# Strassen-type weight sums turned into additions, two of the four in the first MLP matrix made by accumulating DMA transfers

## Chip, cores and metric

The kernel runs on one core of one Trainium2 chip. The metric is the device time of one execution in microseconds (us), the median of three runs. A profiled execution gives the traces quoted below; its times are those of that one execution.

## What is computed

One decoder layer on a sequence of 512 tokens with 2048 channels, all in float32:

```
h = rmsnorm(x, g_mix)
z = h @ w_in                     # 2048 x 10248: conv B, C, V | Q, K, V | forget logits | two gates
conv_branch = (cb * causal_dwconv(cc * cv, conv_w)) @ w_conv_out
attn_branch = forgetting_attention(q, k, v, log_f) @ w_attn_out
merged = sigmoid(gate_c + b) * conv_branch + sigmoid(gate_a + b) * attn_branch
x = x + merged @ w_mix_out
h = rmsnorm(x, g_mlp)
u = square(relu(h @ w_ff1))      # w_ff1: 2048 x 8192
x = x + u @ w_ff2                # w_ff2: 8192 x 2048
out = rmsnorm(x, g_final)
```

## The kernel before

**Products.** Every float32 product is made from float32r parts: an operand is split into a high part (`th`, by ScalarE, line 101) and the rest (`tl`, by VectorE, line 102), and TensorE multiplies high by high, rest by high, and high by rest. A split of one 128 x 2048 tile is therefore one ScalarE and one VectorE instruction, in this order, and TensorE starts a product when `th` is there and needs `tl` for its last third. There are two `th` and two `tl` buffers, so that a split can run at most two products ahead of TensorE.

**Seven products for eight.** The matrix `w_in` (class `Group`, from line 164), `w_ff1` (the same class through `ff1`, line 720) and `w_ff2` (function `unit`, line 770) are multiplied by the Strassen-Winograd scheme: each block of weights is cut into four quarters `X[i, j]`, and seven products named A11, A12, S4, S2, S3, S1 and A22 take the place of eight. Four of the seven weight operands are sums of quarters, made by VectorE in place, 128 x 2048 each (lines 240 to 244 in `Group.tail`): first `X00 = X01 - X00`, then `X01 = X11 - X01`, then `X11 = X11 - X00` (the operand of S2) and `X10 = X10 - X11` (the operand of A22). The second is the operand of S3, the first that of S1. The matching sums of the activations are made in `Quarters.sums` (line 368), and for the second MLP matrix in `put_u` (lines 691 to 698), where the squared activations are combined in seven arrays `r`, split into `rh` and `r`, and stored to DRAM in `s_d` (lines 703, 704).

**A group.** One `Group` is 2 x 256 columns of weights. `head` loads X00 and X10 and makes A11 and A12; `tail` loads X01 and X11 and makes S4, S2, S3, S1, A22. The quarters have four SBUF slots of 1 MiB, handed on through the list `free`: the next group's X00 takes the slot of X11, its X10 that of X01, its X01 that of X00, its X11 that of X10, each as soon as the last split that reads it is done. All these loads are issued by SP (line 178), in the order X00, X10, X01, X11. For `w_ff1` there are 16 groups: four heads first (while the token blocks are still being normalised), then their four tails, then twelve whole groups. `later` holds work that a group leaves to the next tail.

**POOL's queue** carries, in the `w_ff1` stage, the writes and reads of `c_d` (lines 710, 689: a quarter of the activations that is kept in DRAM for a while) and the stores to `s_d`, two pairs of 896 KB for each group. `r` and `rh` have one buffer each, so the next set of sums waits until the store before it has landed.

**Order.** The program is written engine by engine in program order, and a scheduler of the framework then moves instructions within an engine's queue; each engine runs its queue in order.

Of the kernel before, what the change touches and what calls it, by code (L numbers as in the profile page):

```python
# [8 lines left out]
F32 = mybir.dt.float32  # L9
# [3 lines left out]
ALU = mybir.AluOpType  # L13
AX = mybir.AxisListType

P = 128
S = 512
# [3 lines left out]
HS = S // 2  # L21
# [14 lines left out]
V1W = (AW // 2 + NH) // 2  # L36
QSCALE = float(P) ** -0.5
WBUF, SHIFT, PAD = 33 * 64, 16, 16


ORDER = ("A11", "A12", "S4", "S2", "S3", "S1", "A22")
# [4 lines left out]
def tile_hybrid_block(ctx: ExitStack, tc, x, g_mix, w_in, b_f, b_gate, conv_w, w_conv_out,  # L46
                      w_attn_out, w_mix_out, g_mlp, w_ff1, w_ff2, g_final, out):
    nc = tc.nc
    x, out = x[0], out[0]
    w_in, w_conv_out, w_attn_out, w_mix_out = w_in[0], w_conv_out[0], w_attn_out[0], w_mix_out[0]  # L50
    w_ff1, w_ff2 = w_ff1[0], w_ff2[0]
# [3 lines left out]
    main = ctx.enter_context(tc.tile_pool(name="main", bufs=1))  # L55
# [10 lines left out]
    def pair(i, dt, name):  # L66

        return main.tile([P, 2, D], dt, tag=f"t{i}", name=name)
# [35 lines left out]
    def sub(out, a, b):  # L104
        nc.vector.tensor_tensor(out=out, in0=a, in1=b, op=ALU.subtract)  # L105

    def add(out, a, b):
        nc.vector.tensor_tensor(out=out, in0=a, in1=b, op=ALU.add)  # L108

    def parts(shape, at=0):  # L110

        q, w = shape[1:]
        return tuple(main.tile([P, WBUF], F32R, tag=tag, name=tag, bufs=2)[:, at:at + q * w]
                     .rearrange("p (q c) -> p q c", q=q) for tag in ("th", "tl"))
# [49 lines left out]
    class Group:  # L164

        def __init__(self, view, c1, c2, w, ST, mm, banks, put, scale=1.0):
            self.view, self.cs, self.w, self.ST, self.mm, self.banks = view, (c1, c2), w, ST, mm, banks
            self.put, self.scale, self.at = put, scale, {}  # L170

        def load(self, i, j):

            t = main.tile([P, KT // 2, self.w], F32, tag=f"x{free[0]}", name=f"x{i}{j}")
            self.at[i, j] = free.pop(0)
            c = self.cs[j]
            src = self.view[:, c:c + self.w].rearrange("(q two p) c -> two p q c", two=2, p=P)
            nc.sync.dma_start(out=t, in_=src[i])
            return t

        def acc(self, which):
            return [bank(i, which) for i in self.banks["abcd".index(which)]]
# [16 lines left out]
        def plus(self, s, ps, scale=1.0):  # L199

            if len(ps) == 1:
                pairs = [(s, ps[0][:, :2 * self.w].rearrange("p (b c) -> p b c", b=2))]
            else:
                pairs = [(s[:, b, :], ps[b][:, :self.w]) for b in range(2)]
            for o, p in pairs:
                if scale == 1.0:
                    add(o, p, o)
                else:
                    nc.vector.scalar_tensor_tensor(out=o, in0=p, scalar=scale, in1=o, op0=ALU.mult, op1=ALU.add)

# [18 lines left out]
        def tail(self):  # L229
            if self.at:  # L230
                X = self.X
            else:
                X = {(i, 0): self.load(i, 0) for i in range(2)}
            X[0, 1], X[1, 1] = self.load(0, 1), self.load(1, 1)
            a = self.a
            c = self.acc("c")
            self.run(c, "S4", X[1, 1], True)
            while later:
                later.pop(0)()
            sub(X[0, 0], X[0, 1], X[0, 0])  # L240
# [85 lines left out]
    class Quarters:  # L326
# [353 lines left out]
    def put_u(g):  # L680
# [5 lines left out]
        def sums(j):  # L686
            r = pf.tile([P, 7, HS], F32, tag="r", name="r")
            if j == 0:
                nc.gpsimd.dma_start(out=r[:, 0:6:5], in_=c_d[g])
# [10 lines left out]
            nc.scalar.activation(out=h, in_=r, func=AF.Copy)  # L700
            nc.vector.tensor_tensor(out=r, in0=r, in1=h.bitcast(F32), op=ALU.subtract)
            q = 2 * (g % 2) + j
            nc.gpsimd.dma_start(out=s_d[g // 2][:, :, 0, q, :], in_=h.bitcast(F32))
            nc.gpsimd.dma_start(out=s_d[g // 2][:, :, 1, q, :], in_=r)
# [65 lines left out]
    def unit(seg, cg, ST):  # L770
# [4 lines left out]
            kept[cg] = banks2(2 + cg, "b")  # L775
        b = kept[cg]
        X, at = {}, {}
        for i, j in ((0, 0), (0, 1), (1, 1), (1, 0)):
            at[i, j] = free.pop(0)
            t = main.tile([P, 4, S], F32, tag=f"x{at[i, j]}", name=f"y{i}{j}")  # L780
            c = NW * cg + S * j
            src = w_ff2[seg * 1024:(seg + 1) * 1024, c:c + S].rearrange("(q two p) c -> two p q c", two=2, p=P)
            nc.sync.dma_start(out=t, in_=src[i])
            X[i, j] = t

        def run(ps, n, src, first):
            hi, lo = parts([P, 4, S])
# [98 lines left out]
```

## Time and profile before

| | us |
|---|---|
| median of 3 runs | 2563.29 (2560.9 to 2570.82) |
| the profiled execution, whole | 2564.2 |
| its span, first to last instruction | 2562.5 |
| TensorE busy | 2470.4 |
| VectorE busy | 1910.2 |
| ScalarE busy | 1117.7 |

"Busy" is the time in which an engine has an instruction under way. A window of the trace gives, for a stretch of the span, each engine's busy time with its instructions in brackets, the clock granted to TensorE as a share of full speed, the busy share of the sixteen DMA engines and the rate at which they moved bytes. A timeline row gives start, duration, engine, line, operation, output and inputs, and in square brackets how long the engine stood idle before it and what released it. A load from `w_ff1` is 1 MiB and its tile is called `x`; in `w_ff2` it is called `y`. The `w_ff1` stage runs from about 1245 us to 1912 us of the span: heads to 1285, the four tails to 1418.6, the twelve whole groups after that.

### The profile page before, as it was taken

To read this page: it belongs to the slowest core of one execution; us is meant where nothing else is said; L and a number is where in the kernel's file an instruction comes from. 1 tells how busy PE (TensorE), PEld (TensorE's weight loads), DVE (VectorE), ACT (ScalarE), POOL (GpSimd) and SP (SyncE) were. 2 spreads that over 40 slices of the span, in tenths; PEclk is the share of its full clock that TensorE was granted. 3 is DMA by queue.
4 is the path that set the end of the run, shared out by engine and by line. 5 is a ranking of instruction groups with operands and counts; after the bars stand their busy time and mean duration, and the time that the engine had idled before them with its cause. 6 is when DMAs were issued, how large, how long until landed. Compare 5 with 4: busy or idle time off the path is not lost. (4 is left out here: it accounts for less than half of the span.)

```text
span 2562.5 us, 39034 instructions
## 1 busy us (share of the span) xinstructions
PE 2470.4 (96%) x16957; PEld 2267.2 (88%) x16957; DVE 1910.2 (75%) x1484; ACT 1117.7 (44%) x1060; POOL 113.3 (4%) x166
## 2 busy tenths in 40 slices
PE   8999999999999999999998999999989999999997
PEld 8999899999999988888988999999987787787875
DVE  7877677788776744335887888788878878778787
ACT  6433433344454522224545555555543333333344
POOL 0000000000000000000001111111111000000000
PEclk9999999999999999999999999999999999999999
DMA  7554443457344544535656575756687565655562
GB/s 239 168 195 146 144 136 124 147 190 231 126 144 153 199 142 143 184 109 204 207 180 224 192 238 186 235 182 213 205 322 248 191 241 201 230 171 183 205 223 89
DMA packets 292383, 479.75 MB, mean 187 GB/s; under 512 B 10140, under 2 KB 200692, under 8 KB 286452
## 3 DMA queue, kind: packets, MB, share of 16 engines
q1 hardware_dynamic: 268096, 345.08, 41.8%
q0 software_dynamic: 23248, 131.08, 13.6%
q8 instruction: 133, 2.18, 0.3%
q10 hardware_dynamic: 868, 1.10, 0.1%
q14 instruction: 38, 0.31, 0.0%
HBM read 380.75 MB, written 96.47 MB: 186 GB/s over the span
## 5 line engine op out<-in xcount | busy, mean ns | idle before, releaser
L102 DVE TENSOR_TENSOR tl<-x,th 128x2048 fp32r<-128x2048 f32 (+1 forms) x252 | 575.8, 2289 | 192.3 <-ACT th L101 175.1
L101 ACT ACTIVATE th<-x 128x2048 fp32r<-128x2048 f32 (+1 forms) x252 | 481.9, 1917 | 469.3 <-PE a L138 155.3
L105 DVE TENSOR_TENSOR x<-x,x 128x2048 f32<-128x2048 f32 (+1 forms) x144 | 329.4, 2287 | 41.3 <-DMA x<-in_w_ff_dram 35.0
L136 PE MATMUL a<-S,th 128*128 128x256 f32 x1088 | 262.4, 285 | 33.1 <-ACT th L101 27.3
L101 ACT ACTIVATE th<-y 128x2048 fp32r<-128x2048 f32 x80 | 153.8, 1923 | 287.0 <-DVE y L105 115.7
L138 PE MATMUL a<-S,th 128*128 128x256 f32 x1088 | 259.6, 282 | 0.0
L136 PEld LDWEIGHTS a<-S,th 128*128 128x128 f32 x1088 | 210.1, 193 | 38.0 <-ACT th L101 31.6
L102 DVE TENSOR_TENSOR tl<-y,th 128x2048 fp32r<-128x2048 f32 x80 | 182.8, 2285 | 46.1 <-ACT th L101 46.1
L102 DVE TENSOR_TENSOR tl<-raw,th 128x2048 fp32r<-128x2048 f32 x40 | 91.7, 2293 | 160.4 <-ACT th L101 160.0
L138 PEld LDWEIGHTS a<-S,th 128*128 128x128 f32 x1088 | 210.1, 193 | 0.1
L154 PE MATMUL a<-th,us 128*128 128x512 f32 x512 | 202.3, 395 | 8.0 <-DMA us<-s_d 6.2
L156 PE MATMUL a<-th,us 128*128 128x512 f32 x512 | 200.4, 391 | 0.0
L101 ACT ACTIVATE th<-raw 128x2048 fp32r<-128x2048 f32 x40 | 76.8, 1921 | 193.6 <-PE pt L293 71.4
L136 PE MATMUL c<-S,th 128*128 128x256 f32 x544 | 129.4, 282 | 10.0 <-ACT th L101 10.0
L158 PE MATMUL a<-tl,us 128*128 128x512 f32 x512 | 137.8, 391 | 1.1 <-DVE tl L102 1.1
L140 PE MATMUL a<-S,tl 128*128 128x256 f32 x1088 | 138.4, 278 | 0.0
L140 PEld LDWEIGHTS a<-S,tl 128*128 128x128 f32 x1088 | 130.1, 188 | 0.6
L138 PE MATMUL c<-S,th 128*128 128x256 f32 x544 | 128.7, 281 | 0.0
L136 PE MATMUL b<-A,th 128*128 128x256 f32 x544 | 126.2, 277 | 1.5 <-ACT th L101 1.4
L154 PEld LDWEIGHTS a<-th,us 128*128 128x128 f32 x512 | 96.8, 189 | 34.8 <-ACT th L101 15.0
L138 PE MATMUL d<-S,th 128*128 128x256 f32 x544 | 126.8, 278 | 0.0
L136 PE MATMUL d<-S,th 128*128 128x256 f32 x544 | 126.7, 278 | 0.0
(221 smaller groups left out, 5842.1 us busy)
## 6 DMA issues: line engine op xcount, KB each, us to landing
x<-in_w_in_dram SPq DMA_DIRECT2D x86, 1024.0 KB, 5.7
x<-in_w_ff_dram SPq DMA_DIRECT2D x72, 1024.0 KB, 7.6
y<-in_w_ff_dram SPq DMA_DIRECT2D x64, 1024.0 KB, 6.3
us<-s_d POOLq DMA_DIRECT2D x24, 2048.0 KB, 9.9
s_d<-rh POOLq DMA_DIRECT2D x32, 896.0 KB, 6.7
s_d<-r POOLq DMA_DIRECT2D x32, 896.0 KB, 8.1
raw<-in_w_mix_out_dram SPq DMA_DIRECT2D x24, 1024.0 KB, 5.0
g_d<-o SPq DMA_DIRECT2D x32, 256.0 KB, 2.2
```

The costliest lines, as they stand in the source:

```text
L101: nc.scalar.activation(out=hi, in_=src, func=AF.Copy)
L102: nc.vector.tensor_tensor(out=lo, in0=src, in1=hi.bitcast(F32), op=ALU.subtract)
L105: nc.vector.tensor_tensor(out=out, in0=a, in1=b, op=ALU.subtract)
L136: nc.tensor.matmul(o, hi[:, q, js], Sx[:, 0, q, :], start=first and q == 0 and j == 0, stop=False, skip_group_check=True)
L138: nc.tensor.matmul(o, hi[:, q, js], Sx[:, 1, q, :], start=False, stop=False, skip_group_check=True)
L140: nc.tensor.matmul(o, lo[:, q, js], Sx[:, 0, q, :], start=False, stop=q == nq - 1, skip_group_check=True)
L154: nc.tensor.matmul(o, Sh[:, q, ts], hi[:, q, :], start=begin and q == 0, stop=False, skip_group_check=True)
L156: nc.tensor.matmul(o, Sl[:, q, ts], hi[:, q, :], start=False, stop=False, skip_group_check=True)
L158: nc.tensor.matmul(o, Sh[:, q, ts], lo[:, q, :], start=False, stop=q == nq - 1, skip_group_check=True)
```

## The change

The signs of products are turned, so that the first two weight sums are plain sums of quarters: `X00 = X00 + X01` and `X01 = X01 + X11`, and the other two follow as additions. The activation sums get the opposite sign (`minus(out, a, b)` is -a - b), and the products whose sign is turned are subtracted where they were added (`scale` is negated in `Group`, `into` subtracts for j = 1).

In `w_ff1` alone (`dma=ACC1`), the first two sums are not made by VectorE: GpSimd issues a DMA that reads the second quarter from DRAM again and adds it to the quarter in SBUF. In `w_in` and `w_ff2` (`ACC2` is False) they are VectorE additions as before. In `unit` the load of X01 is put ahead of that of X00.

```diff
+ACC1, ACC2 = True, False
...
+    def minus(out, a, b):
+
+        nc.vector.scalar_tensor_tensor(out=out, in0=a, scalar=-1.0, in1=b, op0=ALU.mult, op1=ALU.subtract)
...
-            self.put, self.scale, self.at = put, scale, {}
+            self.put, self.scale, self.dma, self.at = put, -scale, dma, {}
...
+        def plus_quarter(self, t, i, j, loaded):
+
+            if self.dma:
+                nc.gpsimd.dma_start(out=t, in_=self.quarter(i, j), accum_op=ALU.add)
+            else:
+                add(t, t, loaded)
...
                 if scale == 1.0:
                     add(o, p, o)
+                elif scale == -1.0:
+                    sub(o, o, p)
...
             X[0, 1], X[1, 1] = self.load(0, 1), self.load(1, 1)
+            self.plus_quarter(X[0, 0], 0, 1, X[0, 1])
+            self.plus_quarter(X[0, 1], 1, 1, X[1, 1])
             a = self.a
             c = self.acc("c")
             self.run(c, "S4", X[1, 1], True)
             while later:
                 later.pop(0)()
-            sub(X[0, 0], X[0, 1], X[0, 0])
-            sub(X[0, 1], X[1, 1], X[0, 1])
-            sub(X[1, 1], X[1, 1], X[0, 0])
+            add(X[1, 1], X[1, 1], X[0, 0])
             self.run(a, "S2", X[1, 1], False)
-            sub(X[1, 0], X[1, 0], X[1, 1])
+            add(X[1, 0], X[1, 0], X[1, 1])
...
-            add(H[1, 1], H[1, 0], H[1, 1])
+            sub(H[1, 1], H[1, 1], H[1, 0])
             sub(H[1, 0], H[0, 0], H[1, 0])
-            sub(H[0, 0], H[1, 1], H[0, 0])
-            sub(H[0, 1], H[0, 1], H[0, 0])
+            minus(H[0, 0], H[1, 1], H[0, 0])
+            minus(H[0, 1], H[0, 1], H[0, 0])
...
-            add(r[:, 4, :], low[:, 0, :], r[:, 3, :])
+            sub(r[:, 4, :], r[:, 3, :], low[:, 0, :])
             sub(r[:, 1, :], r[:, 0, :], low[:, 0, :])
-            sub(r[:, 2, :], r[:, 4, :], r[:, 0, :])
-            sub(r[:, 6, :], r[:, 5, :], r[:, 2, :])
+            minus(r[:, 2, :], r[:, 4, :], r[:, 0, :])
+            minus(r[:, 6, :], r[:, 5, :], r[:, 2, :])
...
-        return Group(w_ff1, g * S, g * S + HS, HS, Q2.ST, mm_cols, banks, put_u(g))
+        return Group(w_ff1, g * S, g * S + HS, HS, Q2.ST, mm_cols, banks, put_u(g), dma=ACC1)
...
-        for i, j in ((0, 0), (0, 1), (1, 1), (1, 0)):
+        for i, j in ((0, 1), (0, 0), (1, 1), (1, 0)):
...
-            add(xs, ps, xs)
+            if j == 0:
+                add(xs, ps, xs)
+            else:
+                sub(xs, xs, ps)
...
-        sub(X[0, 0], X[0, 1], X[0, 0])
-        sub(X[0, 1], X[1, 1], X[0, 1])
+        plus_quarter(X[0, 0], 0, 1)
+        plus_quarter(X[0, 1], 1, 1)
...
-        sub(t2, X[1, 1], X[0, 0])
+        add(t2, X[1, 1], X[0, 0])
...
-        sub(t2, X[1, 0], t2)
+        add(t2, X[1, 0], t2)
```

**What the scheduler makes of it.** TensorE's queue is unchanged, and so is the order on every engine up to the `w_ff1` stage (only additions stand where subtractions stood). In a whole group of `w_ff1`, VectorE's queue runs: split A11, three short additions and the `r` sums of the group before, split A12, the `r` split (line 701 before), split S4, `X11 += X00`, `X10 += X11`, a short addition, the first `r` sum of the next set, split S2, three `r` sums, split S3, the `r` split, split S1, split A22. Before, split S2 came ahead of that first `r` sum, and split S3 ahead of the other three. POOL's queue runs: the DMA adding to X01, the DMA adding to X00, a pair of `s_d` stores, the read of `c_d`, the write of `c_d`, the other pair of `s_d` stores. The first of them waits for X01's load, the second for X00's load and for the split of A11. `X11 += X00` on VectorE waits for the DMA that adds to X00; the split of S3 waits for the DMA that adds to X01. In `w_ff2` only the order of two loads differs.

More of the change, by code (lines that the diff above doesn't have):

```diff
@@ L164, in tile_hybrid_block, with __init__ @@
     class Group:
-        def __init__(self, view, c1, c2, w, ST, mm, banks, put, scale=1.0):
+        def __init__(self, view, c1, c2, w, ST, mm, banks, put, scale=1.0, dma=False):
             self.view, self.cs, self.w, self.ST, self.mm, self.banks = view, (c1, c2), w, ST, mm, banks
-            self.put, self.scale, self.at = put, scale, {}
+            self.put, self.scale, self.dma, self.at = put, -scale, dma, {}
         def load(self, i, j):
@@ L175, in load, with quarter @@
             self.at[i, j] = free.pop(0)
+            nc.sync.dma_start(out=t, in_=self.quarter(i, j))
+            return t
+        def quarter(self, i, j):
             c = self.cs[j]
-            src = self.view[:, c:c + self.w].rearrange("(q two p) c -> two p q c", two=2, p=P)
-            nc.sync.dma_start(out=t, in_=src[i])
-            return t
+            return self.view[:, c:c + self.w].rearrange("(q two p) c -> two p q c", two=2, p=P)[i]
+        def plus_quarter(self, t, i, j, loaded):
[3 more added lines that the diff above has]
+                add(t, t, loaded)
         def acc(self, which):
@@ L777, in unit, with quarter, plus_quarter @@
         X, at = {}, {}
-        for i, j in ((0, 0), (0, 1), (1, 1), (1, 0)):
+        def quarter(i, j):
+            c = NW * cg + S * j
+            return w_ff2[seg * 1024:(seg + 1) * 1024, c:c + S].rearrange("(q two p) c -> two p q c", two=2, p=P)[i]
+        for i, j in ((0, 1), (0, 0), (1, 1), (1, 0)):
             at[i, j] = free.pop(0)
[L780 to L784, printed above, removed]
+            X[i, j] = main.tile([P, 4, S], F32, tag=f"x{at[i, j]}", name=f"y{i}{j}")
+            nc.sync.dma_start(out=X[i, j], in_=quarter(i, j))
+        def plus_quarter(t, i, j):
+            if ACC2:
+                nc.gpsimd.dma_start(out=t, in_=quarter(i, j), accum_op=ALU.add)
+            else:
+                add(t, t, X[i, j])
         def run(ps, n, src, first):
@@ L793, in into @@
             xs = xp[i][:, :, c:c + S]
-            add(xs, ps, xs)
+            if j == 0:
+                add(xs, ps, xs)
+            else:
+                sub(xs, xs, ps)
             if last and (i, j) in ends:
```

## The prediction

> **What bounds the kernel now.** I read the page first, then the windows by stage, then who ends TensorE's waits, then one whole group in order of time. The first lines and the windows:
>
> ```profile
> span 2562.5 us, 39034 instructions
> PE 2470.4 (96%) x16957; PEld 2267.2 (88%) x16957; DVE 1910.2 (75%) x1484; ACT 1117.7 (44%) x1060; POOL 113.3 (4%) x166
> ```
>
> ```profile
> 420.00:1000.00 580.00, 577.79 (x4492) 552.02 (x4491) 406.43 (x331) 247.53 (x255) 0.81 (x8) 1.00 0.50 163
> 1285.50:1418.60 133.10, 118.41 (x961) 117.01 (x962) 107.65 (x78) 66.80 (x65) 14.00 (x16) 0.96 0.63 208
> 1418.60:1906.10 487.50, 463.57 (x3986) 460.55 (x3985) 399.66 (x298) 280.13 (x274) 64.53 (x79) 0.99 0.64 214
> 1960.00:2260.00 300.00, 297.35 (x1292) 241.01 (x1291) 245.43 (x133) 103.80 (x54) 9.06 (x17) 1.00 0.59 207
> ```
>
> Columns after the stretch: its length, busy TensorE, weight loads, VectorE, ScalarE, POOL, then granted clock, DMA share, GB/s. TensorE leaves 2.2 us of 580 in `w_in` and 2.7 of 300 in `w_ff2`: nothing is to be had there. In `w_ff1` it leaves 14.7 us of 133.1 in the four tails (second row) and 23.9 of 487.5 in the twelve whole groups (third row), 40.6 us a group. These waits are ended by:
>
> ```profile
> PE a L136 <- ACT th L101: 23.5, 13, 2.9
> PE c L136 <- ACT th L101: 10.0, 3, 4.1
> ```
>
> So mostly a product on bank a starts late for its high part. In one whole group it is S2, and what makes it late is VectorE:
>
> ```profile
> 1663.38 2.29 DVE L105 TENSOR_TENSOR x<-x,x 128x2048 f32<-128x2048 f32 x1 [3.87 <-DMA x<-in_w_ff_dram]
> ...
> 1669.99 2.28 DVE L105 TENSOR_TENSOR x<-x,x 128x2048 f32<-128x2048 f32 x1
> ...
> 1672.53 2.29 DVE L102 TENSOR_TENSOR tl<-x,th 128x2048 fp32r<-128x2048 f32 x1
> 1674.73 2.02 DVE L701 TENSOR_TENSOR r<-r,rh 128x1792 f32<-128x1792 f32 x1
> 1676.67 2.29 DVE L105 TENSOR_TENSOR x<-x,x 128x2048 f32<-128x2048 f32 x1
> ...
> 1681.67 2.29 DVE L102 TENSOR_TENSOR tl<-x,th 128x2048 fp32r<-128x2048 f32 x1
> ```
>
> ```profile
> 1679.05 1.91 ACT L101 ACTIVATE th<-x 128x2048 fp32r<-128x2048 f32 x1 [4.69 <-DVE x L105]
> ```
>
> ```profile
> 1681.01 0.58 PE L136 MATMUL a<-S,th 128*128 128x256 f32 x1 [2.81 <-ACT th L101]
> ```
>
> VectorE waits for the landing of X01 (at 1663.3), then works without a break through X00's sum (1663.38), X01's sum (1669.99), the split of S4, the `r` split and X11's sum (1676.67); ScalarE's high part follows at 1679.05, and S2 starts at 1681.01, 2.81 us late. The change takes the first two out of this row. A pause also costs clock:
>
> ```profile
> 1681.00:1688.10 7.10, 7.09 (x49) 7.09 (x50) 6.68 (x7) 4.97 (x5) 1.31 (x2) 0.77 0.60 176
> 1688.10:1693.54 5.44, 5.44 (x51) 5.44 (x50) 4.23 (x2) 3.93 (x4) 1.53 (x2) 1.00 1.04 337
> ```
>
> The product after the pause ran at a granted clock of 0.77 and took 7.10 us, the next, at 1.00, 5.44: 1.66 us more. Seven products of 5.44 are 38.1 us, the floor of a group; twelve are 457.0, so the 463.57 busy hold 6.6 us of slow clock, four such products.
>
> **The additions taken from VectorE.** 16 groups lose two each:
>
> ```profile
> L105 DVE TENSOR_TENSOR x<-x,x 128x2048 f32<-128x2048 f32 x140 | 320.1, 2286 | 41.3 <-DMA x<-in_w_ff_dram 35.0 <-DMA x<-in_w_in_dram 5.5
> ```
>
> 32 x 2.286 = 73 us of VectorE's time. On the path it can be worth no more than TensorE's waits and slow clock: 487.5 - 457.0 = 30.5 us in the whole groups, and in the tails, whose five products take 27.2 us of 33.3, up to 4 x 6.1 = 24.
>
> **What takes their place: 32 transfers of 1 MiB on POOL's queue.** No transfer in the trace adds. What a plain one costs, and where there is room:
>
> ```profile
> 1643.00:1663.00 20.00, 20.00 (x179) 20.00 (x178) 12.83 (x10) 9.89 (x9) 1.88 (x2) 1.00 0.98 320
> 1664.00:1674.00 10.00, 10.00 (x91) 10.00 (x90) 10.00 (x10) 7.57 (x8) 0.00 (x0) 1.00 0.02 7
> ```
>
> ```profile
> DMA to landing us min/median/max: 4.8/8.7/26.0
> ```
>
> From 1643 to 1663 the DMA engines are full (0.98) and move 320 GB/s: 1 MiB is 1.049 MB / (320/0.98) = 3.2 us of all sixteen. From 1664 to 1674 they are idle (0.02). The last row is of the `s_d` stores: the quickest landed 4.8 us after its issue with 0.875 MiB, 2.8 us of transfer, so 2.0 us are fixed. For an adding transfer the bounds are 3.2 us (the destination is read and added in the shadow of the load) and 9.6 us (read, read and write one after another); I take 6.4, since it must fetch two operands where a load fetches one, and the engines are already full with one. The Trainium skill, Collectives: The Full Stack, section "The bandwidth ceiling: the fold count and why AG ≠ RS ≠ AR", speaks against the change in the same way: reduce-scatter has half the rate of all-gather, not because adding costs cycles but because it reads two sources through one ring; by that price the transfer would be 2 x 3.2 = 6.4 us, and no run here shows it yet.
>
> **On the path.** The first adding transfer (to X01) waits for X01's load, the second (to X00) stands behind it:
>
> ```profile
> 1651.22 0.95 POOL L704 DMA_DIRECT2D s_d<-r  x1 [1.41 <-DVE r L701]
> 1674.65 0.94 POOL L703 DMA_DIRECT2D s_d<-rh  x1 [22.48 <-ACT rh L700]
> 1677.05 0.94 POOL L704 DMA_DIRECT2D s_d<-r  x1 [1.46 <-DVE r L701]
> 1682.53 0.72 POOL L689 DMA_DIRECT2D r<-c_d  x1 [4.55 <-DMA s_d<-r]
> ```
>
> POOL has nothing to issue between 1652.2 and 1674.65, so its waiting there holds nobody up. Both transfers go out at 1663.3 and after, and X00's lands at 1663.3 + 2.0 + 2 x 6.4 = 1678.1, with 0.2 for what is left of X11's load (7 GB/s in that window) 1678.3. X11's sum, ready on VectorE at about 1672.3 without the two additions, then starts at 1678.3, against 1676.67 now: **1.6 us later, not earlier**. (The floor would need it at 1678.2 - 1.91 - 2.29 = 1674.0.)
>
> What is late next: the two `s_d` stores queue behind the adding transfers on the same rings, so they transfer from 1677.3, 5.6 us, and land near 1684 where they landed at 1682.5. In the new order VectorE has an `r` sum that waits for this landing ahead of the split of S2, and the sums that wait for the read of `c_d` (3 us after it) ahead of the split of S3. So split S2 starts at 1684.4 (now 1681.67), split S3 near 1688.7, and with the `r` split ahead of it split S1 ends at 1695.3, which is what lets the next X01 load go:
>
> ```profile
> 1690.74 0.37 SPq L178 DMA_DIRECT2D x<-in_w_ff_dram  x1
> ```
>
> ```profile
> 1702.83 2.29 DVE L105 TENSOR_TENSOR x<-x,x 128x2048 f32<-128x2048 f32 x1 [0.64 <-DMA x<-in_w_ff_dram]
> ```
>
> It went at 1690.74 now, so it would be 4.5 us later. The load took 12.1 us to 1702.8, of which 3.2 + 2.0 are its own; some of the rest is queueing that shrinks when it starts later. A group thus grows by 1.6 (all of it regained) to 4.5 (none); I take 3.0. Twelve groups: 36 us. Each now has a pause of several us, so eight more products run at the slow clock: 8 x 1.66 = 13 us.
>
> Tails: 0.63 x 133.1 / 4 = 21.0 us of DMA work each, and 12.8 more make 33.8, above the 33.3 that a tail lasts, with no gap at all; the loop through X01's load gives 40.6 + 3.0 = 43.6 at most. Middle 38.7, 4 x 5.4 = 22 us.
>
> **The rest.** `minus` takes the scalar form; nearest rows:
>
> ```profile
> L564 DVE SCALAR_TENSOR_TENSOR y<-u,cols,y 128x512 f32<-128x512 f32 x16 | 12.0, 748 | 0.3
> L565 DVE TENSOR_TENSOR y<-cb,y 128x512 f32<-128x512 f32 x8 | 5.5, 688 | 0.1
> ```
>
> 60 ns more for each of 64 `r` sums and, scaled, 0.24 for four large ones: 0 to 5 us, and I take 0, since VectorE would be waiting for transfers. The turned signs elsewhere are the same instructions. In `w_ff2` X00 is loaded second:
>
> ```profile
> 2021.47 0.37 SPq L783 DMA_DIRECT2D y<-in_w_ff_dram  x1
> ```
>
> ```profile
> y<-in_w_ff_dram SPq DMA_DIRECT2D x64, 1024.0 KB, 6.3
> ```
>
> ```profile
> 2032.79 1.92 ACT L101 ACTIVATE th<-y 128x2048 fp32r<-128x2048 f32 x1 [3.51 <-PE b L156]
> ```
>
> The second load of a unit goes at 2021.47 and lands 6.3 later, 5.0 before the split of A11, which TensorE releases at 2032.79. Cost 0; were a load to take the 12.1 us seen above, 16 x 0.8 = 13.
>
> **Sum.** 36 + 13 + 22 = +71 us on the profiled execution's 2564.2: 2635. That execution stands 0.9 above the median of the runs.
>
> **Rivals.** *The adding transfer runs near the pace of a load* (3.2 to 5.2 us). At 3.2 X00's sum lands at 1663.3 + 2.0 + 6.4 + 0.2 = 1671.9, ahead of the 1674.0 that the floor needs, and the whole groups lose their 30.5 us; tails, 21.0 + 6.4 = 27.4 us of DMA beside 27.2 of TensorE, gain 0 to 24. Time 2530. For it: idle engines from 1664 to 1674, just where it fits. Against: two operands. *The break-even*: at 5.6 us X00 lands at 1676.7, where its sum starts now; time 2564. *Three passes, or a slow adder* (9.6 us): 6.4 us more in each loop, 12 x 9.4 = 113, tails at 40.2 to 50.0, middle 45.1, 4 x 11.8 = 47, and 13: +173, 2737. For it: nothing in the trace adds, so nothing bounds it better. That the change doesn't do what it says: VectorE's queue holds 32 instructions fewer and POOL's 32 more, so this one is out.
>
> **How the numbers follow.** The forecast (5.9 to 8 us a transfer) has 0.44, the slow adder 0.19, the break-even (5.2 to 5.9) 0.11, the fast transfer 0.26. Slower by over 0.5%, which is about what a measurement of this kernel can tell from no change, 0.63; faster 0.26; between 0.11. The range reaches from the fast transfer (2530) to just under the slow one, 2730, leaving out some 0.15; the forecast's own is 2598 (1.6 us a group, tails 33.8) to 2672 (4.5 a group, tails 43.6).
>
> **What would show it.** Right: adding transfers that land 8 us or more after the one before them; the first sum on `x` in a group (X11's) waiting on a DMA in nearly every group; a DMA share above 0.85 in the whole groups; TensorE's waits there above 50 us, ended by ScalarE's `th`; clock below 0.97. Wrong: transfers landing 3 to 5 us apart, VectorE's busy share down by 73 us, TensorE without waits in the whole groups. A change of over 5 us outside the `w_ff1` stage would mean that I misread the edits costed at nothing.

## The result, and the profile after

The changed kernel takes 2637.98 us (median, 2633.8 to 2642.36) beside 2567.06 us for the kernel before in the same comparison: a ratio of 1.0272, 95% interval 1.023 to 1.0313, so slower. The forecast was 2635. The profiled execution of the changed kernel took 2633.8 us; its page begins:

```profile
span 2632.1 us, 39094 instructions
PE 2485.1 (94%) x16957; PEld 2281.4 (87%) x16957; DVE 1845.0 (70%) x1452; ACT 1112.0 (42%) x1060; POOL 165.0 (6%) x198
q0 software_dynamic: 56528, 164.64, 21.2%
x<-in_w_ff_dram POOLq DMA_DIRECT2D x32, 1024.0 KB, 13.9
```

VectorE lost 65 us of work (1910.2 before) and the kernel still got 70 us longer. The last row is new: 32 adding transfers, 13.9 us from issue to landing in the median. The windows of the changed kernel by stage (columns as in the prediction): `w_in`, the four tails, the twelve whole groups, the stretch between the last product of `w_ff1` and the first of `w_ff2`, and a piece of `w_ff2`:

```profile
420.00:1000.00 580.00, 575.49 (x4492) 550.51 (x4492) 405.21 (x330) 247.34 (x256) 0.80 (x8) 1.00 0.50 162
1289.62:1440.18 150.56, 120.70 (x961) 119.31 (x962) 92.75 (x71) 66.36 (x65) 26.87 (x24) 0.89 0.86 232
1440.18:1966.13 525.95, 482.07 (x4034) 479.11 (x4032) 353.61 (x273) 274.10 (x273) 100.27 (x101) 0.96 0.90 246
1966.13:1985.01 18.88, 0.00 (x0) 0.03 (x1) 6.63 (x6) 4.72 (x7) 0.54 (x1) 0.59 1.01 424
2014.13:2314.13 300.00, 297.37 (x1292) 241.07 (x1291) 244.89 (x134) 104.97 (x55) 10.89 (x19) 1.00 0.61 217
```

Of the 69.6 us, 17.5 lie in the tails (133.1 before), 32.8 in the whole groups, 12.7 in the pause ahead of `w_ff2` (6.2 before) and 2.5 behind it. The twelve whole groups of the kernel before, to the end of the last product (the prediction's window stopped one product short):

```profile
1418.58:1911.71 493.13, 469.20 (x4034) 465.98 (x4032) 404.94 (x302) 281.74 (x277) 64.53 (x79) 0.99 0.64 217
```

The other 4 us were there before the first tail began; the start of this stage lies anywhere from 1245 to 1263 us in thirteen profiled executions of this study, mostly for a reason that the last section gives. What ends the waits of the whole groups (engine, line, what it waited for; us in all, times, longest):

```profile
DVE x L109 <- DMA x<-in_w_ff_dram: 79.2, 12, 8.5
PE a L143 <- ACT th L102: 39.0, 11, 5.0
```

In each of the twelve groups the first sum on VectorE, X11's, waits for a transfer. One group in order of time, POOL's issues first, then VectorE, then ScalarE and TensorE:

```profile
1703.02 3.18 POOL L193 DMA_DIRECT2D x<-in_w_ff_dram  x2 [14.28 <-DVE r L106]
1706.73 0.99 POOL L721 DMA_DIRECT2D s_d<-rh  x1 [0.53 <-ACT o L702]
```

```profile
1697.15 2.29 DVE L103 TENSOR_TENSOR tl<-x,th 128x2048 fp32r<-128x2048 f32 x1 [3.15 <-ACT th L102]
...
1708.58 2.29 DVE L103 TENSOR_TENSOR tl<-x,th 128x2048 fp32r<-128x2048 f32 x1
1719.34 4.62 DVE L109 TENSOR_TENSOR x<-x,x 128x2048 f32<-128x2048 f32 x2 [8.46 <-DMA x<-in_w_ff_dram]
```

```profile
1721.72 1.91 ACT L102 ACTIVATE th<-x 128x2048 fp32r<-128x2048 f32 x1 [12.70 <-DVE x L109]
```

```profile
1723.68 0.51 PE L143 MATMUL a<-S,th 128*128 128x256 f32 x1 [4.96 <-ACT th L102]
```

X01's load lands at 1702.2. Both adding transfers are issued 0.8 us later, X01's first. (The row names an `r` sum that ended then as the releaser; in the groups where X01's landing is on record, the issue comes 0.6 to 1.0 us after it.) They land at 1712.8 and 1719.2. VectorE has been done since 1710.9; X11's sum starts at 1719.34, and S2 4.96 us late. So it went by the way that the prediction described. Note the first VectorE row: the split of A11, after which X00 may be written, was over at 1699.4, and X00's own load had landed long before, so X00's transfer could have gone 3.6 us ahead of X01's. That gap decides the experiments below.

### The profile page after: what moved, and what is told of

Read it like the earlier page. It is cut to its first block, busy times and chain, and to the rows that moved or that the text cites. A ratio compares the mean times of both kernels' runs of the same rounds, so it can differ in the third digit from the quotient of the medians.

```text
span 2632.1 us, 39094 instructions
## 1 busy us (share of the span) xinstructions
PE 2485.1 (94%) x16957; PEld 2281.4 (87%) x16957; DVE 1845.0 (70%) x1452; ACT 1112.0 (42%) x1060; POOL 165.0 (6%) x198
## 5 line engine op out<-in xcount | busy, mean ns | idle before, releaser
L109 DVE TENSOR_TENSOR x<-x,x 128x2048 f32<-128x2048 f32 (+1 forms) x112 | 256.4, 2290 | 88.9 <-DMA x<-in_w_ff_dram 79.2
L143 PE MATMUL a<-S,th 128*128 128x256 f32 x1088 | 269.3, 289 | 47.1 <-ACT th L102 47.1
L145 PE MATMUL a<-S,th 128*128 128x256 f32 x1088 | 266.2, 287 | 0.0
L143 PEld LDWEIGHTS a<-S,th 128*128 128x128 f32 x1088 | 215.7, 198 | 51.4 <-ACT th L102 51.1
L161 PE MATMUL a<-th,us 128*128 128x512 f32 x512 | 202.3, 395 | 21.0 <-DVE o L109 18.9
L145 PEld LDWEIGHTS a<-S,th 128*128 128x128 f32 x1088 | 215.8, 198 | 0.1
L143 PE MATMUL c<-S,th 128*128 128x256 f32 x544 | 134.1, 289 | 30.7 <-ACT th L102 30.7
L143 PEld LDWEIGHTS c<-S,th 128*128 128x128 f32 x544 | 108.0, 198 | 31.7 <-ACT th L102 31.7
L145 PE MATMUL c<-S,th 128*128 128x256 f32 x544 | 133.2, 287 | 0.0
L143 PE MATMUL b<-A,th 128*128 128x256 f32 x544 | 127.8, 279 | 3.9 <-ACT th L102 3.9
L145 PE MATMUL b<-A,th 128*128 128x256 f32 x544 | 127.7, 279 | 0.0
## 6 DMA issues: line engine op xcount, KB each, us to landing
x<-in_w_ff_dram POOLq DMA_DIRECT2D x32, 1024.0 KB, 13.9
```

Source lines behind the costliest of these rows:

```text
L143: nc.tensor.matmul(o, hi[:, q, js], Sx[:, 0, q, :], start=first and q == 0 and j == 0, stop=False, skip_group_check=True)
L145: nc.tensor.matmul(o, hi[:, q, js], Sx[:, 1, q, :], start=False, stop=False, skip_group_check=True)
L161: nc.tensor.matmul(o, Sh[:, q, ts], hi[:, q, :], start=begin and q == 0, stop=False, skip_group_check=True)
```

## The experiments

Stage times are read from the starts of TensorE's products in each profile: four tails, twelve whole groups, the pause ahead of `w_ff2`. They are of one execution each, and a whole-group time can move by up to 18 us with TensorE's pace (last section). Ratios are to the kernel before, each on the chip of its own comparison; the medians of two rows can be from two chips, so compare the ratios.

| kernel | median us | ratio, 95% interval | tails | whole groups | pause |
|---|---|---|---|---|---|
| before | 2567.06 | | 133.1 | 493.1 | 6.2 |
| changed | 2637.98 | 1.0272 (1.023 to 1.0313) | 150.6 | 526.0 | 18.9 |
| load order back | 2644.43 | 1.0262 (1.0235 to 1.029) | 150.3 | 526.1 | 14.4 |
| VectorE adds | 2577.08 | 1.0004 (0.9979 to 1.0028) | 133.0 | 491.3 | 5.7 |
| plain transfers | 2570.51 | 0.9982 (0.9954 to 1.0009) | 139.5 | 482.1 | 9.2 |
| X01 only | 2587.63 | 1.0041 (1.0018 to 1.0063) | 134.9 | 509.5 | 5.6 |
| X00 only | 2611.46 | 1.0167 (1.0128 to 1.0205) | 147.8 | 518.9 | 7.1 |
| whole groups only | 2617.94 | 1.0187 (1.0146 to 1.0228) | 130.5 | 529.0 | 12.0 |
| X00 first | 2610.71 | 1.0151 (1.0108 to 1.0193) | 150.5 | 495.4 | 18.2 |
| X00 first, inner groups | 2582.1 | 1.004 (1.0019 to 1.006) | 130.5 | 498.4 | 5.7 |
| the same, later `r` sums | 2590.92 | 1.0065 (1.004 to 1.009) | 130.7 | 507.5 | 6.4 |
| X01 only, later `r` sums | 2564.48 | 0.9975 (0.995 to 1.0001) | 131.6 | 482.2 | 6.6 |
| VectorE adds, later `r` sums | 2572.59 | 0.9993 (0.9969 to 1.0018) | 132.7 | 494.5 | 5.8 |
| POOL adds | 2650.24 | 1.0315 (1.0274 to 1.0357) | 148.9 | 518.3 | 5.7 |

**Load order back.**

```diff
-        for i, j in ((0, 1), (0, 0), (1, 1), (1, 0)):
+        for i, j in ((0, 0), (0, 1), (1, 1), (1, 0)):
```

> Only the order of the w_ff2 loads is put back (X00 first, X01 second); all else is as in the changed kernel. Theory (the load order costs the pause between the two stages): in the changed kernel TensorE stands 18.9 us between the last product of w_ff1 and the first of w_ff2, and the split of A11 had waited 20.5 us for X00, the second load. With X00 first it lands ahead of that split; the pause falls from 18.9 to 6 to 9 us and the time by 10 to 13 us, to about 2626. Rival (the landing of us, which must pass the s_d stores behind the adding transfers, sets the start whatever the order): pause and time unchanged, 2634 to 2638. The w_ff1 stage (tails 150.6 us, twelve whole groups 526.0) stays as it is under both.

The pause fell by 4.5 us, not by 10 to 13, and the time does not differ from the changed kernel's. Neither theory had it. In both kernels TensorE's first product of `w_ff2` waits for a sum `o` of the last group, and this sum stands in VectorE's queue behind an instruction that waits for a load of `w_ff2`. In the changed kernel that is the split of A11: it waits for ScalarE's `th`, and `th` waits for X00, the second load (VectorE, then TensorE):

```profile
1978.28 2.29 DVE L103 TENSOR_TENSOR tl<-y,th 128x2048 fp32r<-128x2048 f32 x1 [20.51 <-ACT th L102]
...
1984.22 0.69 DVE L109 TENSOR_TENSOR o<-d,o 128x512 f32<-128x512 f32 x1
```

```profile
1985.01 0.77 PE L161 MATMUL a<-th,us 128*128 128x512 f32 x1 [18.88 <-DVE o L109]
```

With X00 first, A11's split waits 5.5 us instead of 20.5, but X00's sum, which stands ahead of `o` too, now waits for X01:

```profile
PE a L161 <- DVE o L109: 14.4, 1, 14.4
ACT o L725 <- DVE o L106: 12.0, 1, 12.0
DVE y L109 <- DMA y<-in_w_ff_dram: 10.5, 1, 10.5
```

In both kernels the pause is a stretch in which the DMA engines are full (1.01 in the window above, 1.02 here); whichever load goes second is late.

**All sums on VectorE, the other edits kept.**

```diff
-ACC1, ACC2 = True, False
+ACC1, ACC2 = False, False
```

> Both additions of w_ff1 are made by VectorE again, all other edits (turned signs, the scalar form in the r sums, the w_ff2 load order) stay. Theory (the adding transfers are the whole cost of the w_ff1 stage, the sign turns cost nothing): tails 133 us, twelve whole groups 493 us as in the kernel before (changed kernel 150.6 and 526.0), the scalar forms hidden. What is left is the load order at the start of w_ff2: 0 to 10 us, so 2564 to 2575. Rival (the turned signs cost by themselves, 64 scalar forms at 60 ns and 4 us on the path): whole groups 495 to 500, 2570 to 2580 even with a short pause between the stages.

The ratio is 1.0004 and all three stages are those of the kernel before. The turned signs, the 64 scalar forms and the load order cost nothing by themselves.

**The same transfers without the adding.**

```diff
-                nc.gpsimd.dma_start(out=t, in_=self.quarter(i, j), accum_op=ALU.add)
+                nc.gpsimd.dma_start(out=t, in_=self.quarter(i, j))
```

> The 32 transfers on POOL's queue go out in the same places with the same waits and sizes but do not add: they overwrite, so the two sums X00 + X01 and X01 + X11 are left out. Theory A (the second operand is what costs: 102 to 108 ns for a 1024-byte packet where a plain load's takes 46): a transfer takes about 3.2 us, the pair lands 9 to 11 us after X01's landing where the adding pair took 16.2, X11's sum is no longer last, whole groups 38 to 40 us each (457 to 480 for twelve), tails 115 to 125, and the time falls to 2555 to 2575. Rival B (1 MiB more traffic twice per group and POOL's issue of 1.6 to 2.3 us cost, whatever the transfer does): pair lands 13 to 16 us after X01, whole groups 42 to 44, time 2620 to 2640.

The time is that of the kernel before, in the range of theory A. The order on every engine is that of the changed kernel, and the same group looks like this (POOL's issues, then VectorE):

```profile
1670.79 1.78 POOL L193 DMA_DIRECT2D x<-in_w_ff_dram  x2 [13.66 <-issue]
```

```profile
1680.03 2.29 DVE L103 TENSOR_TENSOR tl<-x,th 128x2048 fp32r<-128x2048 f32 x1
1682.36 4.62 DVE L109 TENSOR_TENSOR x<-x,x 128x2048 f32<-128x2048 f32 x2
```

X11's sum follows the split of S4 with no wait: the pair had landed at 1677.0 and 1679.7. So 1 MiB more twice a group, on this queue and at this place, is not what costs; the adding is. In the twelve whole groups (medians) the first plain transfer lands 6.5 us after its issue, the second 2.8 us after the first; with adding 9.8 and 5.6. The data rate, in a window with adding transfers alone (changed kernel) and one with plain ones (this kernel), DMA share and GB/s at the end:

```profile
1708.00:1716.00 8.00, 8.00 (x73) 8.00 (x72) 2.87 (x2) 1.02 (x2) 0.97 (x1) 1.00 1.21 188
```

```profile
1674.00:1678.00 4.00, 4.00 (x36) 4.00 (x35) 3.88 (x5) 4.00 (x4) 0.00 (x0) 1.00 1.00 368
```

188 GB/s beside 368, about half. (The share adds up the times of packets, and passes 1 where packets overlap.) POOL's queue in this kernel (packets, MB, share of sixteen engines):

```profile
q0 software_dynamic: 31952, 164.64, 17.5%
```

For the same bytes it has 24576 packets fewer, 768 for each of 32 transfers: 1 MiB goes as 1024 packets of 1 KB when it adds and as 256 of 4 KB when it does not. The smaller packets alone are not the reason: SP's plain loads from `w_ff1` go in packets of 1 KB too, and in the changed kernel one of these took 46 ns in the median where an adding one took 102. Two parts of the expectation were missed. The tails took 139.5 us where 115 to 125 were expected; four products still wait for the high part of S4, so in the tails the traffic costs 6 us, net of the additions that VectorE no longer makes, and the adding 11 more. The whole groups took 482.1 with hardly a wait, 2 above the range: TensorE kept its slower pace (last section).

**One of the two, X01's.**

```diff
-            if self.dma:
+            if self.dma and (i, j) == (1, 1):
```

> One adding transfer per group is left (X01 = X01 + X11); X00 = X00 + X01 is done by VectorE as before, so X11's sum no longer waits for an adding transfer. Theory (X11's sum is late because X00's transfer stands second on the queue behind X01's, and the DMA engines are over-full with both): X11's sum starts 2.3 us earlier than in the kernel before, since only X01's sum leaves VectorE ahead of it; whole groups 39 to 41 us (468 to 492 for twelve), tails 130 to 138, the pause between the stages between 6 and 19: time 2555 to 2575. Rival (one adding transfer, 5.5 us of engines for 1 MiB, already pushes the s_d stores and the next loads back far enough): whole groups 42 to 43, time 2600 to 2620.

Between the two in time, 2587.6; the whole groups, 509.5, are the rival's (42 to 43 us each). X11's sum is in time now; the wait of S2 on `th` is gone from the list of TensorE's waits in the whole groups, and two others stand there:

```profile
PE a L143 <- ACT o L208: 18.3, 10, 4.1
PE d L147 <- DVE tl L103: 10.3, 5, 3.3
```

One such place on ScalarE:

```profile
1674.33 1.71 ACT L718 ACTIVATE rh<-r 128x1792 fp32r<-128x1792 f32 x1 [5.16 <-DVE r L113]
1675.94 1.90 ACT L102 ACTIVATE th<-x 128x2048 fp32r<-128x2048 f32 x1
1677.75 0.57 ACT L208 ACTIVATE o<-a 128x512 f32<-128x512 f32 x1
```

The copy of S2's result, which the next product on that bank needs, is queued behind `rh`, which waits for the `r` sums, which wait for the read of `c_d` behind the late `s_d` stores. The stall moved to the next thing that hangs on POOL's queue.

**The other one, X00's.**

```diff
-            if self.dma:
+            if self.dma and (i, j) == (0, 1):
```

> One adding transfer per group is left, the other one: X00 = X00 + w01 from DRAM; X01 = X01 + X11 is done by VectorE. Measured so far: an adding transfer with nothing ahead lands 9.7 us after its issue, a second one 5.3 us later. Theory (in the changed kernel X11's sum is late because X00's transfer stands second): X00's transfer goes out once A11's split has read X00, some 4.4 us after X01's landing, and lands 14 us after it where the pair took 16 to 17; the floor of a group allows 10.7. S2 is 1 to 4 us late; twelve whole groups 485 to 510 us (changed kernel 526.0, kernel before 493.1), tails 133 to 140; 2565 to 2595 in all. Rival (the load on the DMA engines sets the length, whichever of the two is left): as with X01 alone, whole groups 505 to 515, and 2585 to 2595 with the same waits on VectorE's r sums.

Whole groups 518.9 and tails 147.8: beyond both ranges. The transfer lands 10.7 us after its issue in the median, so it does not stand second any more, but in the whole groups TensorE has both kinds of wait: 11.1 us on `th` (9 times, at most 1.9) and 16.4 on the copy `o` (12 times). Taking one transfer away also let the planner change the order on VectorE, in this kernel and in X01 only alike: three `r` sums stand ahead of the split of S3 where the kernel before has one. Beside the kernel before, the two runs therefore say little about the transfer alone.

Beside each other they explain the tails, 147.8 and 134.9. S4 waits there for the load of X11. X00's transfer is issued ahead of that load, X01's behind it. For the third tail X00's went out at 1339.84 us and the load at 1346.00, and the load took 14.4 us to land; in X01 only the load went at 1353.48, the transfer at 1357.89, and the load took 8.1 us. In the same place it took 7.8 us in the kernel before and 15.3 in the changed one.

**The whole groups only.**

```diff
-        return Group(w_ff1, g * S, g * S + HS, HS, Q2.ST, mm_cols, banks, put_u(g), dma=ACC1)
+        return Group(w_ff1, g * S, g * S + HS, HS, Q2.ST, mm_cols, banks, put_u(g), dma=ACC1 and g > 3)
```

> Adding transfers in the twelve whole groups only; the four tails add on VectorE as before. Theory (the two stages' costs add): tails back to 133 us (150.6 in the changed kernel), whole groups 526, pause between the stages 15 to 19: 17 us less than the changed kernel, 2617 to 2625. Rival (the tails' backlog of transfers is carried into the whole groups, or the reverse): whole groups move by more than 10 us from 526, time below 2610 or above 2630.

2617.9, tails 130.5, whole groups 529.0: the costs of the two stages add up, as the theory had it. The pause, 12.0, is shorter than the 15 to 19 expected.

**X00's transfer first.** The change's own statements stand in the order X00, X01; the planner had put X01's ahead in all twelve whole groups.

```diff
+            if n == "A11":
+                self.low = lo
...
             self.plus_quarter(X[0, 0], 0, 1, X[0, 1])
+            if self.dma and late:
+                e = X[0, 1][:, 0, 0:1]
+                nc.vector.scalar_tensor_tensor(out=e, in0=self.low[:, 0, 0:1], scalar=0.0, in1=e, op0=ALU.mult, op1=ALU.add)
             self.plus_quarter(X[0, 1], 1, 1, X[1, 1])
```

> Both adding transfers in the whole groups, in the other order on POOL's queue: a VectorE instruction of one column, which adds zero times A11's low part to X01, makes X01's transfer wait for A11's split, so that X00's goes first. Values are unchanged. Theory (what costs is that X00's transfer, on which X11's sum waits, stands second): X00 lands 9.7 us after A11's split instead of 15 us after X01's landing, 2.5 to 4 us earlier; whole groups 40.5 to 41.5 each (486 to 500 for twelve), time 2600 to 2612. Rival (the DMA engines, at a share of 0.90, set the length of a group; the order only changes who waits): whole groups 515 to 530, time 2625 to 2640.

Whole groups 495.4: the order alone gives back 30.6 of the 32.8 us, as the theory said, with every byte still moved and added. But for the twelve one-column instructions the order on every engine is that of the changed kernel. TensorE's pace is not the gain: 32 of the 84 products took 5.65 us here, 15 in the changed kernel. One group, POOL's issues and VectorE:

```profile
1695.92 1.58 POOL L193 DMA_DIRECT2D x<-in_w_ff_dram  x1 [8.81 <-DVE tl L103]
1700.26 1.58 POOL L193 DMA_DIRECT2D x<-in_w_ff_dram  x1 [2.76 <-DVE x L258]
```

```profile
1707.93 2.29 DVE L103 TENSOR_TENSOR tl<-x,th 128x2048 fp32r<-128x2048 f32 x1
1710.26 4.62 DVE L109 TENSOR_TENSOR x<-x,x 128x2048 f32<-128x2048 f32 x2
1714.80 0.68 DVE L109 TENSOR_TENSOR o<-b,o 128x512 f32<-128x512 f32 x1
1718.07 0.42 DVE L106 TENSOR_TENSOR r<-r,o 128x256 f32<-128x256 f32 x1 [2.59 <-ACT r L707]
1718.41 2.29 DVE L103 TENSOR_TENSOR tl<-x,th 128x2048 fp32r<-128x2048 f32 x1
```

X00's transfer goes as soon as A11's split has read X00, 4.3 us ahead of X01's, and X11's sum waits for nothing. What is left is in the last two rows: the split of S2 stands behind an `r` sum that waits for a late `s_d` store, so that S2's low part is late by up to 2.8 us in eleven groups (15.3 us in all). Only after the two longest of these waits, 2.3 and 2.8 us, did the next product run at a lower granted clock (0.84 and 0.81).

**The same in the first eleven whole groups only**, VectorE adding elsewhere (`dma=ACC1 and 3 < g < 15`).

> X00's transfer first, adding transfers in the first eleven whole groups only; the four tails and the last whole group add on VectorE; the r sums stand where the planner put them. This is the kernel with three edits without its third. Theory (the costs of the change add up by stage: tails 17 us, pause between the stages 12, order on POOL's queue 31): against X00 first everywhere (2610.7) the tails give back 18 to 20 us and the pause 12, so 2577 to 2584, tails 130 to 133, whole groups 492 to 500, pause 6. Rival (the later r sums had helped, and the group's length is set by the DMA engines): whole groups 505 to 515 as in the kernel with three edits, 2590 and over.

2582.1, tails 130.5, whole groups 498.4, pause 5.7: in the theory's range. With the last group adding on VectorE the pause is that of the kernel before, so the longer pause belongs to the adding transfers of that group, and to both together: with one of them it was 5.6 and 7.1 (the two kernels above with one transfer a group). Placed well, 22 adding transfers cost 0.4%; they still gain nothing.

**The same with the `r` sums later.** The sums, and the squares ahead of them, are tied to the split of S3 in the same way:

```diff
-            while later:
+            while later and not late:
                 later.pop(0)()
...
             self.run(d, "S3", X[0, 1], True)
+            while later:
+                later.pop(0)(self.low["S3"])
...
+            if low3 is not None:
+                e = low[:, :, 0:1]
+                nc.vector.scalar_tensor_tensor(out=e, in0=low3[:, 0:2, 0:1], scalar=0.0, in1=e, op0=ALU.mult, op1=ALU.add)
```

> X00's transfer first, as in the run before, and three edits: the four tails and the last whole group add on VectorE, and the r sums of the whole groups (with the squares on ScalarE ahead of them) stand behind the split of S3 instead of ahead of the splits of S2 and S3, by a one-column VectorE instruction that adds zero times S3's low part; values unchanged. Theory (with X00 first what is left in a whole group is the split of S2, kept on VectorE behind an r sum that waits for the s_d store queued behind both transfers: products waiting for tl 15.3 us in eleven groups, plus the slow clock after each): whole groups 38.1 to 39.5 each (457 to 475 for twelve, or 475 to 493 where TensorE keeps the slower of its two paces, 5.65 us a product), tails 130 to 133, pause 6: 2530 to 2560. Rival (the DMA engines, 0.90 of 43.8 us = 39 us of work a group, become the bound): whole groups 40 to 41.5 and waits on loads, 2560 to 2580.

A miss: 2590.9, beyond both ranges. Nor is it clearly worse than without this edit: the ratios are 1.0065 and 1.004, with intervals that overlap, and of the 9.1 us more in the whole groups some 4.6 are TensorE's pace (38 products at 5.65 us beside 16). The wait for `tl` is gone, and 21.8 us on the copy `o` (11 times) has come in its place. ScalarE's `rh` waits 30.1 us for the later `r` sums, and the copy is behind it in the queue.

**X01 only with the later `r` sums.**

> Only X01's sum by an adding transfer, X00's on VectorE, in the twelve whole groups; tails add on VectorE; r sums behind the split of S3, as in the run beside it. Theory (with X01 alone X11's sum is in time, and what is left is ScalarE and VectorE held by the r chain: 18.3 us on the copy of S2's result, 10.3 on the low part of S3): those waits go, whole groups 38.1 to 39.5 (457 to 475, or 475 to 493 at TensorE's slower pace), tails 130 to 133, pause 6, 2530 to 2560, the same as the run beside it or better. Rival (the later r chain makes its own copies and stores late in the next group): whole groups 500 and over, 2580.

Here the waits do go:

```profile
1433.40:1915.55 482.15, 476.69 (x4034) 476.00 (x4032) 384.29 (x302) 280.28 (x276) 83.72 (x91) 0.99 0.84 248
```

TensorE is busy for 476.7 of 482.2 us. But it made 72 of its 84 products in 5.65 us instead of 5.44, and so the twelve groups took 10.9 us less than before, not some 30: in the range given for the slower pace (475 to 493). The median, 2564.5, is above the 2530 to 2560 expected, and 0.25% below the kernel before, with an interval that reaches 1.0001: not a difference that can be told.

**VectorE adds, with the later `r` sums.**

> No adding transfers, r sums behind the split of S3: the control for the two runs beside it. Theory (without transfers S2 is late because VectorE makes both sums ahead of X11's; the r sums do not matter): whole groups 488 to 495, time within 0.5% of the kernel before, 2560 to 2580. Rival (the later r chain is the gain, whoever adds): whole groups 460 to 478, 2540 to 2555.

As in the theory, nothing: 0.9993.

**X01's sum on POOL's own adder**, X00's on VectorE, no adding transfer:

```diff
-                add(t, t, loaded)
+                (nc.vector if (i, j) == (0, 1) else nc.gpsimd).tensor_tensor(out=t, in0=t, in1=loaded, op=ALU.add)
```

> No adding transfer: X00's sum on VectorE, X01's sum on POOL's own adder (128x2048), the rest as in the changed kernel. No run shows the duration of such an addition on POOL; the nearest row is a MEMSET of 128x512 at 529 ns, so 2 to 5 us. Theory (VectorE's row of work ahead of X11's sum is what makes S2 late): POOL's sum runs beside the splits of A12 and S4 and is done before X11's sum is due; X11's sum starts up to 2.3 us earlier than in the kernel before, whole groups 39 to 40 (468 to 480 for twelve), tails 125 to 133, time 2545 to 2562. Rival (the two engines slow each other when they add at once, or POOL's sum takes over 6 us): X11's sum waits on POOL, whole groups 493 and over, time 2565 to 2600.

The rival's way, and worse than its range: 2650.2. The edit also reaches the groups of `w_in`, where it costs too. The addition takes 4.6 us here, in the range, but VectorE stands still beside it. POOL, then VectorE:

```profile
1689.92 4.62 POOL L195 TENSOR_TENSOR x<-x,x 128x2048 f32<-128x2048 f32 x1 [12.48 <-DMA x<-in_w_ff_dram]
```

```profile
1689.36 0.68 DVE L106 TENSOR_TENSOR o<-o,c 128x512 f32<-128x512 f32 x1
1689.96 4.86 DVE L106 TENSOR_TENSOR r<-r,o 128x256 f32<-128x256 f32 x1
1694.74 0.68 DVE L109 TENSOR_TENSOR o<-d,o 128x512 f32<-128x512 f32 x1
```

An `r` sum that takes 0.42 us elsewhere took 4.86, until POOL was done. The Trainium skill, SBUF — State Buffer, section "Who interferes with whom", states that a VectorE instruction with two SBUF inputs contends with a GpSimd instruction that reads SBUF. The trace agrees.

## Why the prediction was right, point by point

**The mechanism** was right. The additions leave VectorE's row, and what takes their place, X00's transfer, ends later than VectorE would have. That the adding is the price, and not the bytes or the queue, is shown by the plain transfers (ratio 0.9982). That the harm comes through X00's transfer standing second is shown by X00 first (whole groups 495.4 instead of 526.0).

**The landing of X00** was forecast 15.0 us after X01's, as 2.0 fixed, twice 6.4 and 0.2 for the rest of a load. Measured from the first issue it was 15.6, but as 9.8 and 5.6: the part of a transfer that does not scale was 4.2 instead of 2.0, and the pace 5.6 instead of 6.4. Two errors of opposite sign met, and that is luck: 5.6 lies in the band that the prediction gave to the break-even (5.2 to 5.9), not in the forecast's own (5.9 to 8). At this pace the break-even, with its fixed 2.0, would have said 2564; it falls with the fixed part alone. The Trainium skill, Collectives: The Full Stack, section "The bandwidth ceiling: the fold count and why AG ≠ RS ≠ AR", has a reduce-scatter, which reads two sources, at half the rate of an all-gather. The runs agree for this transfer: 2 x 2.8 of the plain one is 5.6. The 6.4 was too high because the 3.2 of a plain transfer was.

**Whole groups**: forecast 36 + 13 = 49 us, measured 32.8. The 13 held: TensorE's busy time grew by 12.9 us (469.20 to 482.07), though the products at a granted clock under 0.8 went from 4 to 10 only, not to 12. The 36 was mis-sized: TensorE's idle time grew by 20.0 us (23.9 to 43.9), 1.7 a group, close to the lower end of the 1.6 to 4.5 out of which 3.0 had been taken. In the groups shown S2 was 4.96 us late where 2.81 had been. The floor of the gain was also misread: the window that ended at 1906.1 left out the last product of the twelfth group, so a group took 41.1 us before, not 40.6, and 36 us stood above the floor, not 30.5.

**Tails**: forecast 22, measured 17.5; 37.6 us each, inside the bounds of 33.8 to 43.6 and near the middle taken. The DMA share there is 0.86. TensorE's wait for the high part of S4 grew from 10.0 us to 30.0, and the load of X11, for which that split waits, comes behind X00's transfer (X00 only, above).

**The step that failed** is that nothing outside the `w_ff1` stage would cost anything. The pause grew by 12.7 us and 2.5 followed it. The new load order is not the reason by itself. With it, and VectorE adding, the pause was 5.7; under the adding transfers, putting the order back took off only 4.5, too little to show in the time. With the last whole group adding on VectorE the pause was 5.7 again. The prediction had read its 5.0 us of room from a unit in the middle of `w_ff2`. In the first unit the second load took 12.2 us even before, and 24.8 in the changed kernel: it was issued 6.4 us later, with the stores to `s_d` and the reads of `us` beside it, and landed 10.1 us after the last product of `w_ff1` where it had landed 8.9 us ahead of it. The forecast had counted what a group's transfers do to the next group and forgot that the last group's next is `w_ff2`.

This miss of 15 made up for most of the 16 and 4.5 by which the two stages were overrated, and the 4 us ahead of the tails, which executions at one pace of TensorE differ by anyway (1245 to 1250, last section), for most of the rest. That 2635 came so near to the measured time is therefore luck.

**Costed at nothing and right**: the turned signs, `minus`, and the load order without adding transfers (ratio 1.0004).

**What was to show it**: X11's sum waits on a DMA in 12 of 12 groups, the DMA share is 0.90 and the clock 0.96, as foretold. TensorE's waits in the whole groups are 44 us, not over 50, and the transfers land 5.6 us apart, not 8.

**What the prediction did not see**: it took the order on POOL's queue as part of the price. X00 was free 3.6 us before X01 had landed, and a third way was open, the same transfers at the same pace in the other order, worth 31 us.

What stays open: how much of the whole groups in X01 only and X00 only (509.5 and 518.9) is the transfer and how much the planner's new order on VectorE.

## What to carry to other kernels

A DMA that adds is not a load with the addition thrown in: here it ran at half the rate and took 3.3 us longer to its first landing, so it fits only where the engines have twice the idle time of a plain load. Before such a transfer is given up or taken, read which instruction is waiting for which of them and put that one first on its queue; here the order of two instructions was worth 31 us and all the turned signs nothing. And when the waits of one stage are filled with transfers, count the stage that comes after the last one.

## What the runs showed of the hardware

**Two paces of TensorE at the same granted clock.** In an unbroken row of products, one product of 48 matmuls follows the other after either 5.44 or 5.65 us, and hardly ever anything else; the granted clock reads 1.00 in both. The pace holds until TensorE pauses, be it for less than 1 us, and can change there. One product of the kernel before and one of X01 only with later `r` sums:

```profile
1500.19:1505.63 5.44, 5.44 (x50) 5.44 (x49) 5.04 (x5) 4.59 (x7) 0.00 (x0) 1.00 0.20 69
```

```profile
1600.48:1606.13 5.65, 5.65 (x50) 1.00 0.96 220
```

(The second window is of TensorE alone.) It is not the kernel's doing. In `w_in` the changed kernel and the one with the load order back have the same instructions in the same order, and the same 360 us held 3156 matmuls in the one and 3059 in the other:

```profile
500.00:860.00 360.00, 357.92 (x3156) 357.52 (x3155) 281.69 (x183) 172.87 (x170) 0.70 (x7) 1.00 0.50 159
```

```profile
500.00:860.00 360.00, 360.00 (x3059) 360.00 (x3058) 270.60 (x176) 168.93 (x159) 0.71 (x7) 1.00 0.50 156
```

Nor is it the chip's: the kernel with plain transfers, which has these instructions too and ran on the chip of the one with the load order back, held 3164. This is most of why the start of the `w_ff1` stage moves by up to 18 us from one execution to another. In the five executions with at most 6 of the products ahead of it at 5.65 us it lies at 1245 to 1250 us, in the eight with 58 to 86 at 1258 to 1263. It also took much of the gain from the two kernels that had removed the waits (plain transfers, and X01 only with later `r` sums): they made 82 and 72 of their 84 products at 5.65 (84 x 0.21 = 18 us). What sets the pace was not found.

**A transfer that adds** goes out in 1 KB packets where the same transfer without adding goes in 4 KB, at 188 GB/s where that moves 368, and its issue occupies POOL for 1.6 us (median 1592 ns) where the plain one's takes 0.9.
